# Turning x and B to tokens by VectorE and DRAM instead of TensorE in a hybrid Mamba-2 layer

## The chip, the cores and the metric

The kernel runs on one core of a Trainium2 chip. The metric is the device time of one execution in microseconds. A core has TensorE (PE), VectorE (DVE), ScalarE (ACT), GpSimd (POOL) and SyncE (SP); each works through its own queue of instructions in order. SyncE, ScalarE and GpSimd also issue the DMAs, each from its own queue.

## The reference

One layer of a hybrid decoder on 320 tokens (a new sequence of 256 and 8 continued sequences of 8), in float32. The model width is 2048. A mixer runs two head groups side by side on one input projection, a gated MLP over chunks of 128 tokens and a state-space part (SSD) of 32 heads in four groups; then comes a convolutional feed-forward part of width 5632.

```python
proj = rms_norm(x) @ w_in            # [gate u | gate v | z | x, B, C | dt]
xbc = silu(causal_depthwise_conv(xbc))            # x: 2048 columns, B and C: 4 groups x 128
xdt = x * dt                                      # (tokens, heads, 64)
cb = einsum("bctgn,bcsgn->bctsg", C, B)
y_diag = einsum("bctgr,bcsgrp->bctgrp", cb * decay, xdt)
states = einsum("bcsgn,bcsgr,bcsgrp->bcgrpn", B, decay_states, xdt)
# states of the chunks and the given initial states are chained with their decays
y_off = einsum("bctgn,bcgrpn,bctgr->bctgrp", C, states_in, exp(da_cs))
y = (y_diag + y_off + d_skip * x) * silu(z)       # then a norm over each group
x = x + rms_norm(concat(gate_out, y) @ w_out)
x = x + rms_norm(conv_ffn(rms_norm(x)))
```

The products over tokens (`states`, `y_diag` and the update of each continued sequence's state) need x·dt and B with tokens on the partitions. The projections deliver x, B and C with channels on the partitions.

## The kernel before

**Weights.** Each weight matrix streams in slabs of 512 KB. `slab` loads one (`wraw`, SyncE, L118), ScalarE rounds it to `whi` (L124), VectorE makes the remainder `wlo` (L125). There are three buffers of each. A slab feeds 24 matmuls of `accumulate`: every fp32 product is done as three products of rounded parts (high·high L153, high·low L154, low·high L155; in the projections of v L144). These matmuls, into the PSUM tiles `ps` (projections) and `pd` (products with `w_out`, `w_down`), make up nearly all of TensorE's work.

**Order.** A scheduler orders every engine's queue by priority. The program runs through the projections in sequence; other work is written as generators in a list `bg`, which are advanced a step at a time between slabs. The sequence is: v; B and C with their convolutions (into `bT`, `cT`: channels by tokens); dt and its sums; x of group 0 (`heads_in(0)`, about 200 to 250 us); the gate stage (`gate_up`, `gate_mix`, about 250 to 430 us, with three products by `w_out`); then the pool `sd` is opened for the SSD. Task `ssd(g)` for each of the four groups g runs in `bg` beside `heads_in(g + 1)`, a product by `w_out` and `heads_out` (about 430 to 750 us). The feed-forward part takes the rest.

**Names around the change.**
- `by_token` (L414): a TensorE transpose of 128x128 by the identity into PSUM. For B there are 16 at the start of `sd` (`bt_ps`), for x 16 in each group (`xt_ps`): two chunks of 128 prompt tokens and two halves of the 64 sample tokens, with four blocks of channels each.
- `fourfold` (L418): a ScalarE copy that repeats 32 sample tokens four times along the free axis, so that the transpose has them on all four partition blocks.
- `btok`, `bsp`: B by tokens for the prompt and, split into two rounded parts, for the samples; written from PSUM by ScalarE (and L807 on VectorE for the remainder).
- `times` (L845): VectorE multiplies x by tokens, from PSUM, by dt into `xdt` and `xq`; `decayed` (L851): POOL multiplies by the decay into `xde`; `xsp` (L862, L863): the samples' x·dt in two rounded parts.
- `with_c(i)` (L908): eight matmuls that multiply state i's two tiles (loaded by `load_state`, SyncE, L830, 256 KB each) by C into `yo_ps`; `shrunk` (POOL, L919) then decays the state, `picked` (ScalarE) selects B of the sequence, `grown` multiplies B and `xsp` (TensorE, L925, `up_ps`) and adds the product to the state (VectorE, L927), `store_state` writes it out. States 0 to 3 are visited one after the other, so `with_c` stands in four places of TensorE's order.
- `decays` and `products`: the masks (tiles `cs`, three buffers, L993) and the matmuls of `y_diag` and `y_off` (`y_ps`, L1004); `final`: the prompt's last state (`fin_ps`, L1032).
- `tp` tag "pv": four buffers of 128x320, shared by several steps that evict PSUM.
- the VectorE adds into `acc_mix` (L249) empty the PSUM tiles `pd`, and so free them for TensorE.

Of the kernel before, what the change touches and what calls it, by code (L numbers as in the profile page):

```python
# [9 lines left out]
F32 = mybir.dt.float32  # L10
# [3 lines left out]
ALU = mybir.AluOpType  # L14
# [3 lines left out]
P = 128  # L18
NP = 256
# [15 lines left out]
def hybrid_step(  # L35
# [21 lines left out]
    def misc(name):  # L57
        return ms.tile([P, 512], F32, tag="ms", name=name)
# [114 lines left out]
    def finish(task):  # L173
        while task in bg:
            tick()
# [233 lines left out]

    TOK = ((0, P), (P, P), (NP, NS))  # L410

    def by_token(ps, x, c):

        pe.transpose(ps, x[:, P * c:P * c + P], ident)  # L414

    def fourfold(out, x, i):

        act.copy(out.rearrange("p k (q t) -> p k q t", q=4), x[:, :, NP + 32 * i:NP + 32 * i + 32].unsqueeze(2).to_broadcast([P, 4, 4, 32]))  # L418
        return out

    with ExitStack() as mctx:
        op = mctx.enter_context(tc.tile_pool(name="op", bufs=1))
# [153 lines left out]
        with tc.tile_pool(name="gp", bufs=1) as gp:  # L576
# [193 lines left out]
            conv_proj(B0, 16, lambda j: bT[:, j, :], rooms[0])  # L770
            conv_proj(C0, 20, lambda j: cT[:, j, :], rooms[1])
            bg.append(tasks)
            x0 = heads_in(0, rooms[0])
            finish(normed)
            uf = gate_up(0)
            for g in range(4):
                res = []
                mix = gate_mix(g, uf, res)
                bg.append(mix)
                if g < 3:  # L780
                    uf = gate_up(g + 1)
                    finish(mix)
                    chunk_out(w_out, g, *res, g == 0)
# [4 lines left out]
        with tc.tile_pool(name="sd", bufs=1) as sd:  # L788
# [4 lines left out]
            cb, cms = shared[:, :NT + NS], shared[:, NT + NS:].rearrange("p (b i) -> p b i", b=NB)  # L793
            pool.tensor_copy(cb[:NS, :NS], ident[:NS, :NS])
            pool.tensor_copy(cb[NS:, NT:], ident[NS:, NS:])
            for c in range(4):
# [4 lines left out]
                if c < 2:  # L801
                    act.copy(btok[:, c, :], ps)
                else:
                    b = bsp[:, c - 2]
                    act.copy(b, ps)
                    for rs in (slice(32, 64), slice(96, P)):
                        dve.tensor_tensor(out=b[rs], in0=ps[rs], in1=b[rs].bitcast(F32), op=ALU.subtract)  # L807

            def by_head(ap):
                return ap.rearrange("p (h d) -> p h d", d=64)  # L810
# [9 lines left out]
            def ssd(g):  # L820
# [5 lines left out]
                def load_state(i):  # L826

                    st = [sd.tile([P, 512], F32, tag="st", name="st", bufs=6) for _ in range(2)]
                    for h in range(2):
                        sp.dma_start(st[h], state_ssm[4 * h + i, g])  # L830
                    return st
# [8 lines left out]
                sts = [load_state(i) for i in range(3)]  # L840

                xdt = sd.tile([P, 3, 512], F32, tag="xdt", name="xdt", bufs=1)
                def times(out, ps, c, at=slice(0, P), h=slice(0, 8)):
                    n = h.stop - h.start
                    dve.tensor_tensor(out=by_head(out), in0=by_head(ps),  # L845
                                      in1=dt[at, c, h0 + h.start:h0 + h.stop].unsqueeze(2).to_broadcast([at.stop - at.start, n, 64]), op=ALU.mult)

                xsp = sd.tile([P, 2, 512], F32R, tag="xsp", name="xsp", bufs=1)
                def decayed(i, c):
# [3 lines left out]
                    return xde  # L853

                def x_of_samples(i):
                    ps = misc("xt_ps")
                    x4 = fourfold(sd.tile([P, 4, P], F32, tag="xde", name="x4", bufs=2), xs, i)
                    for j in range(4):
                        by_token(ps[:, P * j:P * j + P], x4[:, j], 0)
                    xq = sd.tile([P, 512], F32, tag="xde", name="xq", bufs=2)  # L860
                    times(xq, ps, 3 + i)
                    act.copy(xsp[:, i], xq)  # L862
                    dve.tensor_tensor(out=xsp[64:, i], in0=xq[64:], in1=xsp[64:, i].bitcast(F32), op=ALU.subtract)  # L863
                    for r in range(2):
                        at = slice(64 - 64 * r + 32 * i, 96 - 64 * r + 32 * i)
                        times(xdt[at, 2, 256 * r:256 * r + 256], ps[at, 256 * r:256 * r + 256], 2, at, slice(4 * r, 4 * r + 4))

                for c in range(2):
                    ps = misc("xt_ps")
                    for j in range(4):  # L870
# [25 lines left out]
                ps = misc("s1_ps")  # L896
                pe.matmul(ps, btok[:, 0, bs], x0d, start=True, stop=True)
                s1 = sd.tile([P, 512], F32, tag="s1", name="s1", bufs=1)
                act.copy(s1, ps)

                ps_yo = misc("yo_ps")

# [39 lines left out]

                def begin(i):
                    with_c(i, sts[i])
                    bms[i] = picked(i)
                    shrunk(i, sts[i])

                def end(i, by=act):
# [1 line left out]
                    store_state(i, sts[i], by)  # L950
                    return made

                for i in range(4):
                    if i < 3:
                        begin(i)
                    else:
# [59 lines left out]
                for j in range(5):  # L1016
                    for i in range(2):
# [30 lines left out]
            def heads_out(g, rate, later):  # L1048

                ssq = hp.tile([P, NT], F32, tag="ssq", name="ssq")  # L1050
                y = x_of.pop(g)
# [384 lines left out]
```

## Time and profile before

| | |
|---|---|
| Median of 3 runs | 1774.73 us (1774.29 to 1776.76) |
| Profiled execution | 1774.69 us, span 1773.0 us |
| TensorE clock granted | 0.999 |
| TensorE busy | 1765.1 us (100%) |
| VectorE busy | 1173.7 us (66%) |
| ScalarE busy | 817.9 us (46%) |
| GpSimd busy | 274.5 us (15%) |
| moved by DMA | 290 MB, 164 GB/s |

All times of a profile are in microseconds from the start of the span, and engines are named PE, DVE, ACT, POOL and SP in it; L414 is line 414 of the kernel before. Matmuls overlap: a row gives the time of one from its start to its end, the chain of waits gives what it adds to the path. In a list of waits the columns are the total, the count and the longest. In a table of stretches each engine has its busy time and its count of instructions, and the last three columns are the granted clock, the share of the DMA engines and GB/s. In a row of DMA issues the columns are the count, the size of one and the median time from issue to landing.

### The profile page before, as it was taken

To read this page: it belongs to the slowest core of one execution; us is meant where nothing else is said; L and a number is where in the kernel's file an instruction comes from. 1 tells how busy PE (TensorE), PEld (TensorE's weight loads), DVE (VectorE), ACT (ScalarE), POOL (GpSimd) and SP (SyncE) were. 2 spreads that over 40 slices of the span, in tenths; PEclk is the share of its full clock that TensorE was granted. 3 is DMA by queue.
4 is the path that set the end of the run, shared out by engine and by line. 5 is a ranking of instruction groups with operands and counts; after the bars stand their busy time and mean duration, and the time that the engine had idled before them with its cause. 6 is when DMAs were issued, how large, how long until landed. Compare 5 with 4: busy or idle time off the path is not lost.

```text
span 1773.0 us, 30633 instructions
## 1 busy us (share of the span) xinstructions
PE 1765.1 (100%) x11897; PEld 1711.9 (97%) x11897; DVE 1173.7 (66%) x2015; ACT 817.9 (46%) x1193; POOL 274.5 (15%) x602
## 2 busy tenths in 40 slices
PE   9999999999999999999999999999999999999998
PEld 7789999999999998999999999999999999999998
DVE  7549764657978778678865465656657575656575
ACT  5434555334564556445645334343434343333445
POOL 1202200000331313103211011010102010101004
PEclk9999999999999999999999999999999999999999
DMA  7556645455666666555554554555455544454542
GB/s 261 161 150 171 189 141 159 153 152 182 223 189 195 186 203 188 147 179 158 171 158 147 154 153 148 155 148 153 150 151 158 144 156 145 156 155 145 155 151 102
DMA packets 217297, 290.01 MB, mean 164 GB/s; under 512 B 19264, under 2 KB 146624, under 8 KB 216960
## 3 DMA queue, kind: packets, MB, share of 16 engines
q1 hardware_dynamic: 205424, 268.84, 50.1%
q10 hardware_dynamic: 10016, 14.16, 2.2%
q0 software_dynamic: 1712, 5.05, 1.0%
q8 instruction: 94, 1.54, 0.4%
q14 instruction: 51, 0.42, 0.1%
HBM read 273.17 MB, written 14.84 MB: 162 GB/s over the span
## 4 chain that ended last, share of the span: by engine, by line
PE 98%; DVE 1%; issue 0%; ACT 0%; ACTq 0%; DVEq 0%
PE ps L153 19%; PE ps L154 19%; PE ps L155 19%; PE pd L153 10%; PE pd L155 10%; PE pd L154 10%; PE ps_v L144 7%; PE y_ps L1004 1%; PE up_ps L925 0%; PE sg L752 0%; PE yo_ps L908 0%; PE xt_ps L414 0%; PE early L70 0%; PE x1p L1299 0%; DVE xsp L863 0%
## 5 line engine op out<-in xcount | busy, mean ns | idle before, releaser
L125 DVE TENSOR_TENSOR wlo<-wraw,whi 128x1024 fp32r<-128x1024 f32 (+1 forms) x476 | 582.3, 1223 | 421.4 <-ACT whi L124 419.6
L124 ACT CAST whi<-wraw 128x1024 fp32r<-128x1024 f32 (+1 forms) x475 | 495.1, 1042 | 714.5 <-PE ps L154 381.5
L153 PE MATMUL ps<-h_hi,whi 128*128 128x320 f32 x2268 | 700.6, 309 | 0.0
L154 PE MATMUL ps<-h_lo,whi 128*128 128x320 f32 x2268 | 699.3, 308 | 0.0
L155 PE MATMUL ps<-h_hi,wlo 128*128 128x320 f32 x2268 | 698.9, 309 | 0.0
L153 PEld LDWEIGHTS ps<-h_hi,whi 128*128 128x128 f32 x2268 | 425.7, 188 | 2.5 <-issue 1.6
L154 PEld LDWEIGHTS ps<-h_lo,whi 128*128 128x128 f32 x2268 | 425.8, 188 | 0.7
L155 PEld LDWEIGHTS ps<-h_hi,wlo 128*128 128x128 f32 x2268 | 425.6, 188 | 0.0
L155 PE MATMUL pd<-fhi,wlo 128*128 128x320 f32 x704 | 217.0, 308 | 0.0
L153 PE MATMUL pd<-fhi,whi 128*128 128x320 f32 x704 | 217.0, 308 | 0.0
L154 PE MATMUL pd<-flo,whi 128*128 128x320 f32 x704 | 217.0, 308 | 0.0
L153 PE MATMUL pd<-ohi,whi 128*128 128x320 f32 x448 | 139.1, 310 | 0.0
L155 PE MATMUL pd<-ohi,wlo 128*128 128x320 f32 x448 | 138.4, 309 | 0.0
L154 PE MATMUL pd<-olo,whi 128*128 128x320 f32 x448 | 138.1, 308 | 0.0
L153 PEld LDWEIGHTS pd<-fhi,whi 128*128 128x128 f32 x704 | 132.2, 188 | 0.0
L154 PEld LDWEIGHTS pd<-flo,whi 128*128 128x128 f32 x704 | 132.2, 188 | 0.0
L155 PEld LDWEIGHTS pd<-fhi,wlo 128*128 128x128 f32 x704 | 132.2, 188 | 0.0
L1201 POOL COPY ptf<-pad 128x2 f32<-128x2 f32 x88 | 21.0, 238 | 602.7 <-DVE pad L1189 601.9
L249 DVE TENSOR_TENSOR acc_ffn<-acc_ffn,pd 128x320 f32<-128x320 f32 (+1 forms) x161 | 77.5, 482 | 37.8 <-PE pd L155 36.3
L153 PEld LDWEIGHTS pd<-ohi,whi 128*128 128x128 f32 x448 | 84.1, 188 | 1.6 <-issue 1.0
L154 PEld LDWEIGHTS pd<-olo,whi 128*128 128x128 f32 x448 | 84.1, 188 | 0.3
L155 PEld LDWEIGHTS pd<-ohi,wlo 128*128 128x128 f32 x448 | 84.1, 188 | 0.2 <-issue 0.2
(335 smaller groups left out, 1866.5 us busy)
## 6 DMA issues: line engine op xcount, KB each, us to landing
wraw<-in_ffn_w_up SPq DMA_DIRECT2D x176, 512.0 KB, 3.6
wraw<-in_w_in SPq DMA_DIRECT2D x140, 512.0 KB, 3.8
wraw<-in_ffn_w_down SPq DMA_DIRECT2D x88, 512.0 KB, 3.3
wraw<-in_w_out SPq DMA_DIRECT2D x64, 512.0 KB, 3.4
st<-in_state_ssm SPq DMA_DIRECT2D x32, 256.0 KB, 4.1
out_ssm_state_sample<-st ACTq DMA_DIRECT2D x30, 256.0 KB, 4.1
cs<-dacs_d SPq DMA_DIRECT2D x16, 320.0 KB, 4.7
xr<-in_xT SPq DMA_DIRECT2D x4, 640.0 KB, 4.0
```

The lines of the kernel that those rows point to most:

```text
L124: rounded[:] = [act.copy(hi, raw).ins]
L125: dve.tensor_tensor(out=lo, in0=raw, in1=hi.bitcast(F32), op=ALU.subtract)
L144: made = pe.matmul(out, xi, w[g][wi], start=first and begins, stop=last and ends)
L153: pe.matmul(ps, whi, xhi, start=first, stop=False)
L154: pe.matmul(ps, whi, xlo, start=False, stop=False)
L155: return pe.matmul(ps, wlo, xhi, start=False, stop=last).ins
L249: added_last[:] = [dve.tensor_tensor(out=acc[:, nb, ts], in0=acc[:, nb, ts], in1=ps[:, ts], op=ALU.add).ins]
L1004: pe.matmul(ps[64 * i:64 * i + 64, cols], w(hl), x(hl, m, cpx), tile_position=(0, 64 * i), **flags)
L1201: pool.tensor_copy(ptf[:, k, :], pad[:, 256:258])
```

## The change

x of each group and B are turned to tokens without TensorE. `to_tokens` takes 64 tokens at a time: one VectorE transpose of 32x32 blocks over 128x256 into a "pv" buffer, then four DMAs from GpSimd's queue that write 64 rows of 512 bytes each to a scratch tensor in DRAM (`b_d`, `x_d[g]`). A tensor takes five such pieces, so 5 transposes and 20 DMAs. `from_dram` reads back 128 tokens by 512 channels through GpSimd's queue, for the samples with a broadcast that repeats 32 tokens four times; a tensor takes four such reads of 256 KB. The rows come back in a permuted order of channels, which `in_order` and the access patterns of `times` undo; `times` becomes two VectorE instructions, which read SBUF. `fourfold` and `by_token` go. B and x of group 0 are written during the gate stage, x of groups 1 to 3 directly behind their convolution in `heads_in_next`; the reads of group g + 1 (three of four) are issued behind the products of group g, into `cs` buffers.

In `ssd` the C products of states 0, 1 and 2 and the first chunk's state product (`state_of_prompt`) stand together in one visit; those of state 3 follow in a second one.

```diff
+    b_d = dr.tile([NT, 512], F32, name="b_d")
+    x_d = [dr.tile([NT, 512], F32, name=f"x_d{i}") for i in range(4)]
...
-    def by_token(ps, x, c):
-        pe.transpose(ps, x[:, P * c:P * c + P], ident)
-    def fourfold(out, x, i):
-        act.copy(out.rearrange("p k (q t) -> p k q t", q=4), x[:, :, NP + 32 * i:NP + 32 * i + 32].unsqueeze(2).to_broadcast([P, 4, 4, 32]))
-        return out
+    def to_tokens(x, rows):
+        for o in range(0, NT, NS):
+            t = tp.tile([P, NT], F32, tag="pv", name="turned", bufs=4)[:, :4 * NS].rearrange("p (r f) -> p r f", r=2)
+            dve.transpose(out=t.rearrange("p r (j f) -> p r j f", j=4), in_=x[:, :, o:o + NS].rearrange("p j (r t) -> p r j t", t=32))
+            for i in range(4):
+                pool.dma_start(rows[o:o + NS, P * i:P * i + P].rearrange("(r t) f -> t r f", t=32), t[32 * i:32 * i + 32])
+            yield
+    def from_dram(out, rows, c):
+        o = P * c if c < 2 else NP + 32 * (c - 2)
+        pool.dma_start(out, rows[o:o + P] if c < 2 else rows[o:o + 32].unsqueeze(0).broadcast_to([4, 32, 512]))
+        return out
...
+            b_turned = to_tokens(bT, b_d)
+            bg.append(b_turned)
             x0 = heads_in(0, rooms[0])
             finish(normed)
+            x0_turned = to_tokens(x0, x_d[0])
+            bg.append(x0_turned)
             uf = gate_up(0)
+            finish(b_turned)
+            for c in range(2):
+                from_dram(b_raw[:, c], b_d, c)
+            finish(x0_turned)
...
+            there = {0: [from_dram(room(), x_d[0], c) for c in range(2)]}
             for c in range(4):
-                ps = misc("bt_ps")
-                b4 = bT if c < 2 else fourfold(sd.tile([P, 4, P], F32, tag="xde", name="b4", bufs=2), bT, c - 2)
-                for g in range(4):
-                    by_token(ps[:, P * g:P * g + P], b4[:, g], c if c < 2 else 0)
...
+                b4 = b_raw[:, c] if c < 2 else from_dram(room(), b_d, c)
+                b = btok[:, c] if c < 2 else bsp[:, c - 2]
+                act.copy(b.rearrange("p (j i f) -> p j i f", j=4, f=32), in_order(b4))
...
+                    for r in range(2):
+                        dve.tensor_tensor(out=to[:, r], in0=of[:, r],
+                                          in1=by[:, r].unsqueeze(2).unsqueeze(3).to_broadcast([n, m, 2, 32]), op=ALU.mult)
...
-                for c in range(2):
-                    ps = misc("xt_ps")
-                    for j in range(4):
-                        by_token(ps[:, P * j:P * j + P], xs[:, j], c)
-                    times(xdt[:, c, :], ps, c)
-                    if c == 0:
-                        x0d = decayed(0, 0)
+                x2, x4 = there[g][:2], there[g][2:]
+                sts = [load_state(i) for i in range(3)]
...
+                times(xdt[:, 0, :], x2[0], 0)
+                x0d = decayed(0, 0)
+                x4 += [from_dram(room(), x_d[g], c) for c in range(2 + len(x4), 4)]
+                yield
+                times(xdt[:, 1, :], x2[1], 1)
                 x_of_samples(0)
                 yield
...
-                for i in range(4):
-                    if i < 3:
-                        begin(i)
-                    else:
+                state_of_prompt(x0d)
+                for i in range(3):
+                    begin(i)
+                yield
+                x_of_samples(1)
+                for i in range(2):
+                    bms[i] = picked(i)
+                yield
+                yield
+                for i in range(3):
+                    end(i)
+                    if i < 2:
+                        bms[i + 2] = picked(i + 2)
+                    if i == 0:
                         sts.append(load_state(3))
-                    if i:
-                        end(i - 1)
                     yield
-                    if i == 0:
-                        x_of_samples(1)
-                    yield
+                yield
                 begin(3)
...
+                if g < 3:
+                    there[g + 1] = [from_dram(room(), x_d[g + 1], c) for c in range(3)]
                 x1d = decayed(1, 1)
...
             def heads_in_next(g):
                 x_of[g] = heads_in(g)
+                for _ in to_tokens(x_of[g], x_d[g]):
+                    pass
                 bg.append(tasks[g])
```

More of the change, by code (lines that the diff above doesn't have):

```diff
@@ L795, in hybrid_step, with room @@
             pool.tensor_copy(cb[NS:, NT:], ident[NS:, NS:])
+            def room():
+                return sd.tile([P, 2, NT], F32, tag="cs", name="xt", bufs=3).rearrange("p i n -> p (i n)")[:, :512]
+            there = {0: [from_dram(room(), x_d[0], c) for c in range(2)]}
             for c in range(4):
-                ps = misc("bt_ps")
-                b4 = bT if c < 2 else fourfold(sd.tile([P, 4, P], F32, tag="xde", name="b4", bufs=2), bT, c - 2)
-                for g in range(4):
-                    by_token(ps[:, P * g:P * g + P], b4[:, g], c if c < 2 else 0)
-                if c < 2:
-                    act.copy(btok[:, c, :], ps)
-                else:
[L804 to L807, printed above, removed]
+                b4 = b_raw[:, c] if c < 2 else from_dram(room(), b_d, c)
+                b = btok[:, c] if c < 2 else bsp[:, c - 2]
+                act.copy(b.rearrange("p (j i f) -> p j i f", j=4, f=32), in_order(b4))
+                for rs in (slice(32, 64), slice(96, P)) if c > 1 else ():
+                    h = b[rs].rearrange("p (j i f) -> p j i f", j=4, f=32)
+                    dve.tensor_tensor(out=h, in0=in_order(b4[rs]), in1=h.bitcast(F32), op=ALU.subtract)
             def by_head(ap):
@@ L838, in load_sums, with times @@
                     return cs
-                sts = [load_state(i) for i in range(3)]
                 xdt = sd.tile([P, 3, 512], F32, tag="xdt", name="xdt", bufs=1)
[L843 to L846, printed above, removed]
+                def times(out, x, c, at=slice(0, P), h=slice(0, 8)):
+                    n, m = at.stop - at.start, (h.stop - h.start) // 2
+                    to = out.rearrange("p (j r i f) -> p r j i f", j=m, r=2, i=2)
+                    of = x.rearrange("p (r i j f) -> p r j i f", r=2, i=2, j=4)[:, :, h.start // 2:h.stop // 2]
+                    by = dt[at, c, h0 + h.start:h0 + h.stop].rearrange("p (j r) -> p r j", r=2)
+                    for r in range(2):
+                        dve.tensor_tensor(out=to[:, r], in0=of[:, r],
+                                          in1=by[:, r].unsqueeze(2).unsqueeze(3).to_broadcast([n, m, 2, 32]), op=ALU.mult)
                 xsp = sd.tile([P, 2, 512], F32R, tag="xsp", name="xsp", bufs=1)
@@ L855, in x_of_samples @@
                 def x_of_samples(i):
-                    ps = misc("xt_ps")
-                    x4 = fourfold(sd.tile([P, 4, P], F32, tag="xde", name="x4", bufs=2), xs, i)
-                    for j in range(4):
-                        by_token(ps[:, P * j:P * j + P], x4[:, j], 0)
                     xq = sd.tile([P, 512], F32, tag="xde", name="xq", bufs=2)
-                    times(xq, ps, 3 + i)
+                    times(xq, x4[i], 3 + i)
                     act.copy(xsp[:, i], xq)
@@ L865, in x_of_samples, with state_of_prompt @@
                         at = slice(64 - 64 * r + 32 * i, 96 - 64 * r + 32 * i)
-                        times(xdt[at, 2, 256 * r:256 * r + 256], ps[at, 256 * r:256 * r + 256], 2, at, slice(4 * r, 4 * r + 4))
-                for c in range(2):
-                    ps = misc("xt_ps")
-                    for j in range(4):
-                        by_token(ps[:, P * j:P * j + P], xs[:, j], c)
-                    times(xdt[:, c, :], ps, c)
-                    if c == 0:
-                        x0d = decayed(0, 0)
+                        times(xdt[at, 2, 256 * r:256 * r + 256], x4[i][at], 2, at, slice(4 * r, 4 * r + 4))
+                s1 = sd.tile([P, 512], F32, tag="s1", name="s1", bufs=1)
+                def state_of_prompt(x0d):
+                    ps = misc("s1_ps")
+                    pe.matmul(ps, btok[:, 0, bs], x0d, start=True, stop=True)
+                    act.copy(s1, ps)
+                x2, x4 = there[g][:2], there[g][2:]
+                sts = [load_state(i) for i in range(3)]
                 ps = misc("cb_ps")
@@ L892, in ssd @@
                                       op=ALU.mult)
+                times(xdt[:, 0, :], x2[0], 0)
[3 more added lines that the diff above has]
+                times(xdt[:, 1, :], x2[1], 1)
                 x_of_samples(0)
                 yield
[L896 to L899, printed above, removed]
                 ps_yo = misc("yo_ps")
@@ L1050, in heads_out @@
                 ssq = hp.tile([P, NT], F32, tag="ssq", name="ssq")
[L1051 removed]
+                y = x_of[g]
                 def z_evac(j, ps):
```

5 lines of the change are left out of this document (3 added, 2 removed).

## Prediction

> **What bounds the kernel now.** I read the page's head, its busy times and its chain first, then the list of TensorE's waits, then the stretches in which the change works.
>
> ```profile
> span 1773.0 us, 30633 instructions
> PE 1765.1 (100%) x11897; PEld 1711.9 (97%) x11897; DVE 1173.7 (66%) x2015; ACT 817.9 (46%) x1193; POOL 274.5 (15%) x602
> PE 98%; DVE 1%; issue 0%; ACT 0%; ACTq 0%; DVEq 0%
> L125 DVE TENSOR_TENSOR wlo<-wraw,whi 128x1024 fp32r<-128x1024 f32 (+1 forms) x476 | 582.3, 1223 | 421.4 <-ACT whi L124 419.6
> L124 ACT CAST whi<-wraw 128x1024 fp32r<-128x1024 f32 (+1 forms) x475 | 495.1, 1042 | 714.5 <-PE ps L154 381.5
> ```
> ```profile
> PE early L70 <- DVE ones L66: 1.1, 1, 1.1
> PE spread L302 <- DVE rs_r L286: 0.7, 2, 0.4
> PE up_ps L925 <- DVE xsp L863: 0.5, 2, 0.2
> PE ps L190 <- ACT h_hi L401: 0.2, 1, 0.2
> ```
> ```profile
> 422.00:504.00 82.00, 81.93 (x610) 76.79 (x609) 67.33 (x112) 51.80 (x102) 23.94 (x33) 1.00 0.68 216
> 504.00:595.00 91.00, 90.74 (x660) 86.02 (x659) 72.29 (x130) 53.52 (x104) 22.51 (x32) 1.00 0.62 190
> ```
> TensorE is busy all the time at a granted clock of 1.00, makes 98% of the chain and waits 2.5 us in all, never for a weight. So a TensorE instruction taken away is time taken away, as long as nothing else then comes late. The stretches (columns: length, PE, PEld, DVE, ACT, POOL) are the state-space stages of groups 0 and 1: VectorE is busy 82% and 79%, close behind. The idle time of the two weight lines says how much lateness is covered: ScalarE's rounding waits mostly for TensorE to free a buffer, so a slab is made as soon as there is room, two slabs ahead. A slab is 24 matmuls at 0.147 us, 3.5 us; two are 7.0, less 1.04 + 1.22 for rounding and remainder: some 4.8 us of cover.
>
> **What is taken from TensorE.** Every L414 matmul goes.
>
> ```profile
> L414 PE MATMUL xt_ps<-ident,xs x32: 271/272/273, 433.6 to 684.9; 128*128 128x128 f32 x32
> L414 PE MATMUL xt_ps<-ident,x x32: 270/272/273, 439.7 to 695.4; 128*128 128x128 f32 x32
> L414 PE MATMUL bt_ps<-ident,bT x8: 271/272/273, 425.5 to 426.7; 128*128 128x128 f32 x8
> L414 PE MATMUL bt_ps<-ident,b x8: 272/273/331, 432.6 to 433.5; 128*128 128x128 f32 x8
> ```
> ```profile
> 504.10 0.87 PE xt_ps L414 x8
> ...
> 509.25 0.15 PE ps L155
> 509.40 0.44 PE xt_ps L414 x4
> 509.84 0.86 PE s_ps L897 x2
> 510.70 0.57 PE yo_ps L908 x8
> 511.27 0.34 PE ps L153
> ```
> The rows of the one line say how many (32 + 32 + 8 + 8 = 80), but their 272 ns overlap; the chain gives what one takes of the path, 0.87 / 8 = 0.109 us. 80 × 0.109 = **8.7 us**. The chain shows a second price: the first weight matmul behind a visit of plain fp32 work takes 0.34 us instead of 0.15, so a visit costs about 0.2 us besides its own matmuls. The matmul orders of the two kernels have 38 such visits in the four groups before and 25 after (the C products of states 0 to 2 and the first-chunk state product now stand in one visit, and visits that held transposes alone are gone): 13 × 0.2 = **2.6 us**. The C products themselves (128) and all other matmuls stay. Together 11.3 us; the visits are few and rounded, so 9.5 to 11.5.
>
> **What is added elsewhere.** VectorE gets 25 transposes of 128x256 and pays the multiplications by dt in two halves, 64 instructions for 32. POOL's queue gets 100 writes of 32 KB and 20 reads of 256 KB. ScalarE loses ten fourfold copies.
>
> ```profile
> L312 DVE STREAM_TRANSPOSE turned<-ssq x4: 505/512/514, 539.1 to 767.8; 128x320 f32<-128x320 f32 x4
> L845 DVE TENSOR_TENSOR xdt<-xt_ps,dt x24: 411/426/692, 438.0 to 701.5; 32x256 f32<-32x256 f32 x16, 128x512 f32<-128x512 f32 x8
> ```
> ```profile
> 83.45 0.54 POOL L711 DMA_DIRECT2D lg<-in_gate_ln_g  x1
> ...
> 85.55 0.56 POOL L738 DMA_DIRECT2D bs<-in_gate_b_s  x1
> ```
> ```profile
> st<-in_state_ssm SPq DMA_DIRECT2D x32, 256.0 KB, 4.1
> wT<-in_gate_wT POOLq DMA_DIRECT2D x4, 256.0 KB, 4.3
> w<-in_gate_w POOLq DMA_DIRECT2D x4, 8.0 KB, 3.4
> bias_bc<-in_ssm_dt_bias POOLq DMA_DIRECT2D x1, 16.0 KB, 5.7
> out_ffn_conv_sample<-stg ACTq DMA_DIRECT2D x22, 32.0 KB, 1.5
> ```
> The nearest transpose, 320 columns, took 0.51 us; 256 of them by columns about 0.43 (estimate). 25 × 0.43 = 10.7 us of VectorE, 2.1 in each tensor. The multiplications: 512 columns 0.69, 256 columns 0.42, so 0.16 fixed and 0.26 for each 256; eight halves at 0.42 and eight at 0.29 against 4 × 0.69 + 4 × 0.42 are +1.3 us a group (nothing to 3, as the operands now come permuted and from SBUF). VectorE's stage of group 1 goes from 72.3 to about 75.7 of 91: still under TensorE, so this costs nothing by its sum.
>
> Five issues on POOL stood 0.53 us apart, so the four writes of one transposed tile take 2.2 us to issue and land after some 3.4, POOL's row for small pieces (1.5 at the least, by ScalarE's row of 32 KB, 5.7 at the most, by POOL's slowest row). B and x of group 0 are written in the gate stage:
>
> ```profile
> 253.71 1.23 DVE L125 TENSOR_TENSOR wlo<-wraw,whi 128x1024 fp32r<-128x1024 f32 x1 [2.30 <-ACT whi L124]
> ...
> 262.07 1.22 DVE L125 TENSOR_TENSOR wlo<-wraw,whi 128x1024 fp32r<-128x1024 f32 x1
> ```
> ```profile
> 262.48 0.58 POOL L736 DMA_DIRECT2D wT<-in_gate_wT  x1 [17.45 <-PE sg L753]
> ```
> POOL stands idle there for 17 us; the 42 issues take 42 × 0.54 = 23 us and end near 268, and the next wT load, issued at 262.5 now, goes behind them, 5 us later; in VectorE's new order its masking stands behind the next projection's evictions, so nobody waits. Six transposes there wait for writes four tiles back, 5.6 us after those start and 2.2 us apart, with a wlo behind some; VectorE idles 2.3 us ahead of a wlo now, and with the slabs' cover I cost this at nothing. If the cover is gone it is the slower rival below.
>
> Where the change adds a wait: the transposes write into the four rooms "pv", so the fifth transpose of a tensor waits until the writes of the first are done, and all of VectorE's queue waits behind it: the adds that free TensorE's accumulators, the products' masks, the next wlo. For group 1, whose fifth transpose comes near 482.6 by VectorE's rows:
>
> ```profile
> 485.40 0.49 DVE L249 TENSOR_TENSOR acc_mix<-acc_mix,pd 128x320 f32<-128x320 f32 x1 [0.55 <-PE pd L155]
> 486.33 0.55 DVE L1014 SCALAR_TENSOR_TENSOR xs<-xs,prm,y_ps 128x320 f32<-128x320 f32 x1 [0.44 <-PE y_ps L1004]
> 489.05 0.49 DVE L249 TENSOR_TENSOR acc_mix<-acc_mix,pd 128x320 f32<-128x320 f32 x1 [0.58 <-PE pd L155]
> 490.81 0.49 DVE L249 TENSOR_TENSOR acc_mix<-acc_mix,pd 128x320 f32<-128x320 f32 x1 [0.47 <-PE pd L155]
> 493.21 1.23 DVE L125 TENSOR_TENSOR wlo<-wraw,whi 128x1024 fp32r<-128x1024 f32 x1 [1.91 <-ACT whi L124]
> ```
> The first tile's writes begin near 480.5, so it waits to 480.5 + 2.2 + 3.4 = 486.1: 3.5 us, plus 2.1 for the transposes. The idle time in these rows gives back 0.55 + 0.44 + 0.58 + 0.47 + 1.91 = 3.95, and the slabs' cover of 4.8 holds the rest; only the accumulators have less. I take 0.4 us for each of groups 1 to 3, **1.2 us** (0 to 2 each).
>
> Group 0's start is the other place. The C products of three states in one visit need all six state loads together.
>
> ```profile
> 438.02 0.37 SPq L118 DMA_DIRECT2D wraw<-in_w_in  x1
> ```
> ```profile
> 441.20 0.64 PE L908 MATMUL yo_ps<-st,cb_cms 128*32 128x256 f32 x8
> ```
> The sixth load stands on SP's queue behind a weight load like this one, which waits for VectorE; issued at 438.4 and landing 4.1 us on, it is there at 442.5. The first state's products start at 441.2; with 0.57 us a state, as in the chain, the visit asks for the third near 442.3 (the transposes taken out ahead of it and the state product put in move that little). I take **0.8 us** (0 to 2). ScalarE there waits for the last of the reads of B, issued when the gate stage's rooms come free near 429.4: four issues and 4.3 us after waiting rooms, near 439.5; with 51.8 of 82 us busy it has to catch up: **0.6 us** (0 to 2). For the later groups the reads are issued a group ahead, into rooms that the products have left; nothing waits for them.
>
> Sum against the profiled execution, 1774.69 us (span 1773.0 and 1.7 around it; the median of three runs is 1774.73): 1774.69 − 8.7 − 2.6 + 1.2 + 0.8 + 0.6 = **1766.0 us**.
>
> A rule that speaks against the change: the Trainium skill, "VectorE: DVE Perf Modes", "Rules for kernel authors", gives a 128×128 transpose to TensorE where PSUM will do as its target, since VectorE turns only 32×32 blocks. By it the kernel before would be the better one; here TensorE is the engine without idle time, and the row of 0.109 us on the path is the measure.
>
> **Rivals.**
> *Nothing waits.* The three waits cost nothing: 1774.69 − 11.3 = 1763.4. For it: TensorE waits only 0.5 us in these stages now. Against: covers of 0.8 us or less at group 0.
>
> *The gain is given back.* VectorE and ScalarE bound the stages: fifth transposes at 2 us each and group 0 at 2 + 2 make 10 instead of 2.6: 1763.4 + 10 = 1773.4. For it: writes that land after 5.7 us, and a VectorE busy to 82%, in bursts. Against: the idle time in the rows of group 1.
>
> *Slower: VectorE held through the "pv" rooms.* If one write takes POOL a whole VectorE instruction (1.22 us, the wlo row) instead of 0.54, four take 4.9, the fifth transpose waits 480.5 + 4.9 + 3.4 = 488.8, which is 6.2 and with the transposes 8.3 us against 3.95 of idle time: 4 us for each of three groups, 13. In the gate stage POOL then needs 40 × 1.22 = 49 instead of 22 us, and the last transposes, with the wlo queued behind them, are late by some 10, less 4.8: 5. 1763.4 + 13 + 5 = 1781. It decides from about 0.9 us an issue. Against it: the wT issue at 262.48 took 0.58 us while a remainder with two SBUF inputs ran beside it. The Trainium skill, "SBUF — State Buffer", "SBUF: two separate sides", has this as a trap: POOL writes its queue's descriptors through a port that certain VectorE instructions hold. By it this rival would be the likely one; that row disagrees.
>
> *The removed work does not shorten the path*: it lay in time in which TensorE would otherwise have waited, 1774. Against: the list of waits.
>
> **How the numbers follow.** Forecast 0.52 (1764.5 to 1769), nothing waits 0.13, given back 0.18, slower 0.13, no effect 0.04. A measurement of this kernel can tell about 0.2%, 3.5 us: faster ends at 1771.2, slower begins at 1778.2. The given-back case spreads from 1769 to 1776, so a third of it is still faster. Faster 0.52 + 0.13 + 0.06 = 0.71; slower 0.13; the same 0.16. The range goes from 1762.5, the upper removal of 11.5 with a little, to 1775.0, over the given-back case; the slower rival is left out.
>
> **What would show it.** Right: no L414; TensorE's busy time down by 11; chain pieces "0.57 yo" no longer alone but joined; waits of TensorE in total under 6 us, at yo_ps near 442 and at the first pd or ps behind each fifth transpose. Wrong: VectorE idle before a transpose for over 6 us, POOL's issues over 0.9 us apart, or TensorE waiting for wlo in the gate stage.

## The result and the profile after

The changed kernel took **1813.97 us** (median of 4, 1812.66 to 1816.59) against 1774.99 us beside it: ratio 1.022 (95% interval 1.0202 to 1.0238). It is 39 us slower where 9 us of gain were forecast.

The head of the page, the busy times and the chain, after:

```profile
span 1812.8 us, 30726 instructions
PE 1770.7 (98%) x11817; PEld 1712.1 (94%) x11817; DVE 1199.2 (66%) x2072; ACT 810.9 (45%) x1183; POOL 341.4 (19%) x722
PE 85%; DVE 6%; DMA 5%; POOL 2%; issue 2%; ACT 1%; SPq 0%; DVEq 0%; POOLq 0%; ACTq 0%
```

The 80 matmuls are gone (11,817 for 11,897), but TensorE has 98% of a longer span, and the chain runs over VectorE and DMAs for 11%. What TensorE waits for most, after (total, count, longest):

```profile
PE up_ps L946 <- DVE xsp L881: 15.0, 4, 6.9
PE yo_ps L929 <- DMA st<-in_state_ssm: 8.2, 7, 2.4
PE up_ps L946 <- DVE st L948: 6.2, 4, 3.1
PE y_ps L1032 <- issue: 1.5, 1, 1.5
PE y_ps L1032 <- POOL cpx L1012: 1.5, 1, 1.5
```

Nearly all of it is work of the state-space groups. The same four stretches of time that hold the four groups before, now after the change, where the groups lie later by what was lost so far (length, PE, PEld, DVE, ACT, POOL, clock, DMA share, GB/s):

```profile
422.00:504.00 82.00, 72.38 (x487) 64.92 (x486) 63.79 (x111) 40.29 (x74) 27.86 (x45) 0.94 0.73 209
504.00:595.00 91.00, 85.92 (x611) 80.64 (x610) 73.24 (x132) 46.32 (x85) 30.63 (x45) 0.98 0.64 198
595.00:683.00 88.00, 79.02 (x527) 73.46 (x526) 62.67 (x110) 38.78 (x74) 31.79 (x39) 0.94 0.64 192
683.00:746.00 63.00, 52.17 (x370) 47.00 (x369) 52.09 (x93) 32.52 (x62) 30.55 (x47) 0.92 0.56 165
```

TensorE is idle for 82 + 91 + 88 + 63 less the four busy times, 34.5 us, where the kernel before has 0.6. And a second cost shows in the clock column, which was 1.00 before: 0.94, 0.98, 0.94 and 0.92. By these shares up to 0.06·82 + 0.02·91 + 0.06·88 + 0.08·63 = 17 us are lost to the clock. Idle time and slow clock, less the 11.3 us that the prediction took from TensorE, come to 40 us, about what was measured.

Two places cost most: the start of group 0 and group 3. Matmul by matmul, the weight products of the kernel after lie 12.5, 20.4, 28.1 and 40.7 us behind those before at the ends of the four stretches.

At the start of group 0 the chain after has this piece (start, length, what):

```profile
435.57 11.92 DMA xt<-b_d
```

The second read of B's samples is issued only at 435.57, since there are three rooms and the first must be emptied by `times`; GpSimd's queue after:

```profile
435.57 0.70 POOL L426 DMA_DIRECT2D xt<-b_d  x1 [3.31 <-DVE xdt L867]
```

The read repeats 32 tokens four times and lands after 11.9 us. ScalarE stands with its copy, and the next rounding of weights with it (ScalarE after, idle time in brackets):

```profile
442.82 0.62 ACT L824 CAST bsp<-xt 128x512 fp32r<-128x512 f32 x1 [7.99 <-DMA xt<-b_d]
447.52 0.62 ACT L824 CAST bsp<-xt 128x512 fp32r<-128x512 f32 x1 [4.08 <-DMA xt<-b_d]
```

The loads of SyncE's own queue are late with it. The DMA issues of 430 to 450 us after, and, last row, of 425 to 450 us before (count, size, time to landing):

```profile
st<-in_state_ssm SPq DMA_DIRECT2D x6, 256.0 KB, 12.0
wraw<-in_w_in SPq DMA_DIRECT2D x2, 512.0 KB, 11.3
xt<-b_d POOLq DMA_DIRECT2D x2, 256.0 KB, 11.6
```
```profile
st<-in_state_ssm SPq DMA_DIRECT2D x6, 256.0 KB, 4.0
```

TensorE waits for the states (after), and its stretches of 4 us there show the clock:

```profile
444.75 0.75 PE L929 MATMUL yo_ps<-st,cb_cms 128*32 128x256 f32 x2 [2.44 <-DMA st<-in_state_ssm]
446.56 2.13 PE L929 MATMUL yo_ps<-st,cb_cms 128*32 128x256 f32 x8 [1.05 <-DMA st<-in_state_ssm]
```

```profile
437.00:441.00 4.00, 4.00 (x28) 3.91 (x27) 2.11 (x3) 0.00 (x0) 1.04 (x2) 1.00 1.01 230
441.00:445.00 4.00, 1.56 (x12) 0.29 (x10) 1.37 (x2) 0.62 (x1) 0.00 (x0) 1.00 1.08 157
445.00:449.00 4.00, 2.64 (x10) 0.37 (x8) 0.81 (x2) 1.48 (x2) 0.68 (x1) 0.51 1.00 192
449.00:453.00 4.00, 2.00 (x10) 1.19 (x11) 3.89 (x9) 2.48 (x6) 0.00 (x0) 0.50 0.69 188
453.00:457.00 4.00, 4.00 (x22) 4.00 (x22) 3.94 (x5) 2.38 (x5) 3.70 (x3) 0.71 0.56 177
```

Behind a stretch in which TensorE works 1.56 of 4 us the granted clock falls to half. The last three rows, 0.51, 0.50 and 0.71, are half rate for 3.9, 4.0 and 2.3 us, some 10.2 us in all, so until near 455.3. TensorE has by then worked without a gap since 452.01, for 3.3 us. The Trainium skill, "TensorE: Matmul & The Clock Gate", "Part 1: The HAM clock gate", states half rate after an idle window of about 3.4 us and full rate after as long a busy one; the trace agrees in size on the way back to full rate, but the rate fell here with no single gap above 2.44 us.

In group 3 the longest of the waits for `xsp` stands, the samples' x·dt; these waits, 15.0 us, are TensorE's largest. VectorE's part of it, the six decays that GpSimd works through meanwhile, and TensorE (after):

```profile
736.88 1.43 DVE L881 TENSOR_TENSOR xsp<-xq,xsp 64x512 fp32r<-64x512 f32 x1
```
```profile
730.26 7.50 POOL L940 TENSOR_TENSOR st<-st,tote 128x512 f32<-128x512 f32 x6
```
```profile
738.37 0.79 PE L946 MATMUL up_ps<-xsp,bm 128*128 128x512 f32 x1 [6.90 <-DVE xsp L881]
```

VectorE's multiplications by dt and this remainder take about two to three times as long beside GpSimd's work as alone; the experiments come back to it.

### The profile page after: what moved, and what is told of

The parts are those of the page before. It is cut to its first block, busy times and chain, and to the rows that moved or that the text cites. A ratio compares the mean times of both kernels' runs of the same rounds, so it can differ in the third digit from the quotient of the medians.

```text
span 1812.8 us, 30726 instructions
## 1 busy us (share of the span) xinstructions
PE 1770.7 (98%) x11817; PEld 1712.1 (94%) x11817; DVE 1199.2 (66%) x2072; ACT 810.9 (45%) x1183; POOL 341.4 (19%) x722
## 4 chain that ended last, share of the span: by engine, by line
PE 85%; DVE 6%; DMA 5%; POOL 2%; issue 2%; ACT 1%; SPq 0%; DVEq 0%; POOLq 0%; ACTq 0%
PE ps L153 16%; PE ps L154 16%; PE ps L155 16%; PE pd L153 9%; PE pd L155 9%; PE pd L154 9%; PE ps_v L144 7%; DVE wlo L125 2%; DMA cs<-dacs_d 1%; POOL x_d L420 1%; DVE cv L460 1%; DMA xt<-b_d 1%; DMA xt<-x_d 1%; DVE xdt L867 1%; DMA st<-in_state_ssm 1%
```

## The experiments

Four kernels of the table (marked *) end, in their profiles, with 6.7 to 7.6 us in which no work is visible: SyncE's last barrier waits there for TensorE's sequencer, 7.5 us at once in the changed kernel without reads (first row; total, count, longest) against 0.9 in the kernel before (second row). No run shows why. It lies behind all of the kernel's work, so beside the medians stands the start of the last addition of a weight product in each profile, as its distance from the kernel before (1756.3). A profile is of one execution, which can lie 3 us from the median.

```profile
SPq L1463 <- PEq L1463: 8.3, 2, 7.5
```
```profile
SPq L1432 <- PEq L1432: 1.1, 2, 0.9
```

| kernel | median us | ratio, 95% interval | last addition |
|---|---|---|---|
| changed kernel | 1813.97 | 1.0202 to 1.0238 | +40.6 |
| merged visits alone | 1789.24 | 1.0065 to 1.0095 | +16.8 |
| merged visits, decays spread | 1789.28 | 1.0062 to 1.0092 | +12.7 |
| tokens by DRAM, four visits | 1812.17 | 1.0195 to 1.0225 | +39.2 |
| the same without reads * | 1799.99 | 1.0126 to 1.0156 | +19.6 |
| ... and without transposes, writes | 1785.14 | 1.0048 to 1.0083 | +10.5 |
| ... and without decays | 1768.52 | 0.9950 to 0.9976 | −4.4 |
| changed kernel without reads * | 1803.41 | 1.0145 to 1.0175 | +20.7 |
| changed kernel without decays | 1799.23 | 1.0121 to 1.0155 | +25.6 |
| prompt alone by DRAM * | 1794.70 | 1.0095 to 1.0125 | +15.6 |
| before with multiplications from SBUF | 1784.16 | 1.0039 to 1.0069 | +9.5 |
| the same without decays | 1776.38 | 0.9996 to 1.0015 | +1.6 |
| before without decays | 1773.57 | 0.9979 to 0.9998 | −0.5 |
| before with transposes and writes * | 1790.61 | 1.0072 to 1.0102 | +8.4 |
| changed kernel, plain reads | 1797.74 | 1.0107 to 1.0141 | +23.0 |
| plain reads, four visits | 1797.49 | 1.0114 to 1.0144 | +22.4 |
| changed kernel, two writes a piece | 1818.22 | 1.0228 to 1.0258 | +47.9 |

**Taking parts out.** First the reads, or the decays, out of the changed kernel.

```diff
-        pool.dma_start(out, rows[o:o + P] if c < 2 else ...)
-        return out
+        return bT.rearrange("p j n -> p (j n)")[:, :512]
```


> The changed kernel without the reads from DRAM: where x and B by tokens are wanted, the tile bT stands instead (so the results are not the layer's); the transposes, the writes and all arithmetic stay. Theory R (the reads through GpSimd's queue land after 7 to 12 us and hold ScalarE and VectorE): the 13 us of group 0 and the late samples of the others go, 1763 to 1772. Theory D (VectorE's multiplications by dt, now from SBUF, stand beside six GpSimd decays in a row and take three times as long): the 11 us each of groups 2 and 3 stay, 1785 to 1795.


```diff
                     with_c(i, sts[i])
-                    shrunk(i, sts[i])
```


> The changed kernel without GpSimd's decays of the given states (32 multiplications of 128x512 left out, the states are not decayed). Theory D: the multiplications by dt go back to about 0.42 us, the waits at up_ps go, and only group 0 with its 13 us and the waits on the writes are left, 1785 to 1793. Theory R: at least 1805.

Neither median lies in a range of its theories; both gave something back, neither all: 20 us of last addition for the reads, 15 for the decays. Matmul by matmul, the four stretches lose 12.5, 7.9, 7.7 and 12.6 us in the changed kernel and 3.5, 4.5, 4.8 and 8.0 without the reads: most of group 0's loss goes, as theory R said, and more than half of the others' stays. So there is more than one cause.

**The two halves of the change.** The merged visits alone on the kernel before, with the later updates of the states that go with them, and the way through DRAM alone.

```diff
-                for i in range(4):
-                    if i < 3:
-                        begin(i)
...
+                for i in range(3):
+                    begin(i)
+                yield
+                x_of_samples(1)
```


> The kernel before with the second part of the change alone: C products of states 0 to 2 in one visit, TensorE's transposes kept. If the visits are worth their switches and cost no wait: 1774.7 less 8 visits of 0.2 us, about 1773. If six decays in a row and state loads that are wanted together are themselves a cause of the loss: 1778 to 1790.

> The changed kernel with the C products in four visits as before, the way through DRAM kept. Theory R: nearly all of the loss is left, 1800 to 1815. Theory D, in which the order of the new visits puts the decays beside the multiplications: groups 2 and 3 lose little, 1780 to 1790.

Visits alone: 14 us slower, with nothing of the way through DRAM in it. TensorE's waits in that kernel:

```profile
PE yo_ps L908 <- DMA st<-in_state_ssm: 4.8, 4, 2.2
PE up_ps L925 <- DVE st L927: 3.2, 6, 1.2
PE y_ps L1010 <- issue: 2.0, 1, 2.0
```

The states' loads are late, and where the updates of three states follow one another, TensorE waits for the additions that free their PSUM tiles (`up_ps`). All its waits come to 14.7 us, where the kernel before has 2.5, and over 624 to 631 us the granted clock was 0.52; together that is about the loss. The way through DRAM alone costs 37 us; on top of it the merged visits add 2, perhaps because what they would wait for is late already. Were the six decays in a row the reason? (The edit is shown against the merged visits alone.)

```diff
-                    shrunk(i, sts[i])
+                    if i in (0, 3):
+                        shrunk(i, sts[i])
...
+                shrunk(1, sts[1])
                 yield
+                shrunk(2, sts[2])
                 yield
```


> The merged visits on the kernel before, but the decays of states 1 and 2 a slab and two slabs later, as the visits were before. If six decays in a row are what makes the merged visits cost: 1774 to 1779. If it is the six state loads that are wanted at once, and the later sample products: 1786 to 1790.

1789.28 us, the same; not the decays in a row. (Its profiled execution was the fastest of its four, that of the merged visits alone the slowest; hence the different last additions.) Whether the loads or the later updates weigh more was not told apart.

**The way through DRAM, peeled.** With four visits, first the reads left out (bT stands for them), then also the transposes and writes, then also the decays.

```diff
-        for o in range(0, NT, NS):
+        for o in ():
```


> Way through DRAM with the C products in four visits, the reads left out (the tile bT stands for x and B by tokens). Theory R (the reads are what is late): about 1766, as the transposes' 8.7 us are gone and nothing else waits. Theory W (the waits for the writes through the four rooms hold VectorE) or theory D (VectorE's multiplications from SBUF): 1785 to 1795.

> As the kernel without reads in four visits, and VectorE's transposes and their writes left out too: what is left of the change is that TensorE transposes nothing and that the multiplications by dt read SBUF, in two halves. Theory W: 1764 to 1768. Theory D (VectorE's multiplications with two SBUF operands are held by GpSimd's decays): still above 1775.

> The kernel without transposes, writes and reads, and also without GpSimd's decays of the states. Theory D: 1762 to 1766, and 5 to 15 us less than with the decays. If the decays don't matter: the same as with them within 2 us.

By the last addition: reads 39.2 − 19.6 = 19.6 us, transposes and writes 19.6 − 10.5 = 9.1, and 10.5 + 4.4 = 14.9 between decays and none. Theories R, W and D were each a part; none of the low times that one theory alone would have given came. With everything out the kernel is faster than before by 0.24 to 0.50%: the transposes were on the path.

**Single costs, added to the kernel before.** The multiplications from SBUF, with and without the decays:

```diff
-                    times(xq, ps, 3 + i)
+                    times(xq, still, 3 + i)      # still: bT, 512 columns; times in two halves
```


> The kernel before, with one thing added: the multiplications by dt read an SBUF tile (bT, so the values are not the layer's) in two halves, as in the changed kernel; TensorE's transposes stay and nobody reads them. Theory D alone is enough: plus 10 to 17 us, 1785 to 1792, without any DMA. If D needs the other parts: within 3 us of 1775.

> The kernel before with the multiplications by dt from SBUF (values not the layer's), and without the decays. If those multiplications cost because GpSimd's decays and VectorE hold one another up: within 2 us of the control without decays. If it is VectorE's longer work as such: 8 us above it, as with the decays.

> Control: the kernel before without GpSimd's decays of the given states (they are left out). As TensorE waits only 2.5 us in all there, 1773 to 1776.

From SBUF they cost 9.5 us (8.3 by the medians), a little less than expected; without the decays 1.6 + 0.5 = 2.1 over the control (2.8), just above the 2 expected. So some 5 to 7 us of it appear only when the decays run too. TensorE's waits for `xsp` fall with the decays; first with them, then without (total, count, longest):

```profile
PE up_ps L930 <- DVE xsp L868: 5.8, 3, 3.8
```
```profile
PE up_ps L930 <- DVE xsp L868: 1.8, 1, 1.8
```

Taking TensorE's transposes away gains nothing as long as this wait stands: the kernel peeled down to these multiplications, without the transposes, is at +10.5, this one, with them, at +9.5. The groups of VectorE from 428 to 770 us (count, busy, mean ns), before and in the control without decays, then with the multiplications from SBUF, then the same without decays (two rows), and in the changed kernel:

```profile
L845 DVE TENSOR_TENSOR xq<-xt_ps,dt 128x512 f32<-128x512 f32 x8 | 5.5, 686 | 1.2 <-PE xt_ps L414 1.2
```
```profile
L845 DVE TENSOR_TENSOR xq<-xt_ps,dt 128x512 f32<-128x512 f32 x8 | 5.5, 686 | 2.6 <-PE xt_ps L414 2.6
```
```profile
L849 DVE TENSOR_TENSOR xq<-bT,dt 128x256 f32<-128x256 f32 x16 | 11.7, 758 | 0.1
```
```profile
L849 DVE TENSOR_TENSOR xq<-bT,dt 128x256 f32<-128x256 f32 x16 | 7.0, 468 | 0.1
L849 DVE TENSOR_TENSOR xdt<-bT,dt 128x256 f32<-128x256 f32 x16 | 11.0, 726 | 0.0
```
```profile
L867 DVE TENSOR_TENSOR xdt<-xt,dt 32x128 f32<-32x128 f32 x32 | 14.7, 488 | 5.6 <-DMA xt<-x_d 5.3
L867 DVE TENSOR_TENSOR xq<-xt,dt 128x256 f32<-128x256 f32 x16 | 10.2, 656 | 4.0 <-DMA xt<-x_d 4.0
L867 DVE TENSOR_TENSOR xdt<-xt,dt 128x256 f32<-128x256 f32 x16 | 9.0, 607 | 5.2 <-DMA xt<-x_d 5.1
```

From PSUM the decays make no difference, 686 ns with and without. From SBUF half the columns of `xq` take longer than all of them took from PSUM, until the decays go. `xdt` stays slow, 726 ns without the decays: GpSimd's other multiplications (`xde`, `cpx`, `s`) run beside it. The trace of the changed kernel tells the two cases apart, instruction by instruction: of the multiplications of 128x256, the 19 with no arithmetic of GpSimd beside them took 0.41 to 0.43 us each, the 13 with some 0.95 us in the mean and up to 1.28. The samples' remainder, which always had two SBUF operands, shows the same in the kernel before and in the control without decays:

```profile
L863 DVE TENSOR_TENSOR xsp<-xq,xsp 64x512 fp32r<-64x512 f32 x8 | 8.4, 1045 | 0.2
```
```profile
L863 DVE TENSOR_TENSOR xsp<-xq,xsp 64x512 fp32r<-64x512 f32 x8 | 5.5, 690 | 0.2
```

In one place of the kernel with the multiplications from SBUF, VectorE and then POOL:

```profile
694.48 2.50 DVE L849 TENSOR_TENSOR xq<-bT,dt 128x256 f32<-128x256 f32 x2
```
```profile
694.44 2.26 POOL L924 TENSOR_TENSOR st<-st,tote 128x512 f32<-128x512 f32 x2 [5.81 <-PE yo_ps L913]
```

Each of two multiplications lasts 1.25 us, about as long as a decay beside it (1.13). The Trainium skill, "SBUF — State Buffer", "Who interferes with whom", says that a VectorE instruction with two SBUF inputs contends with a GpSimd instruction that reads SBUF, and that one with at most one, outside VectorE's two-port modes, does not; the rows above agree with both.

The transposes and the writes added, read by nobody:

```diff
+                for _ in to_tokens(x_of[g], x_d[g]):
+                    pass
```


> The kernel before, with VectorE's 25 transposes and the 100 writes added, which nobody reads. Theory W: plus 8 to 12 us, 1783 to 1787, with VectorE idle before each fifth transpose. If the writes cost only beside the others: within 3 us of 1775.

8.4 us by the last addition (the median, 14.7 us up and above the expected range, holds the longer end too). The place that cost most, in group 1's products (VectorE, POOL, TensorE):

```profile
579.90 1.09 DVE L418 STREAM_TRANSPOSE turned<-xs 128x256 f32<-128x256 f32 x3
...
587.41 0.45 DVE L418 STREAM_TRANSPOSE turned<-xs 128x256 f32<-128x256 f32 x1 [4.74 <-DMA x_d<-turned]
```
```profile
579.16 4.26 POOL L420 DMA_DIRECT2D x_d<-turned  x8 [1.56 <-DVE turned L418]
585.04 1.06 POOL L420 DMA_DIRECT2D x_d<-turned  x2 [1.61 <-DMA x_d<-turned]
```
```profile
588.68 0.85 PE L1021 MATMUL y_ps<-cs,xdt 128*64 128x128 f32 x6 [2.38 <-DVE cs L1010]
590.87 1.47 PE L1021 MATMUL y_ps<-cs,xdt 128*64 128x128 f32 x8 [1.33 <-issue]
```

The fifth transpose stands 4.7 us for a room, the masks of the products (`cs`) behind it, and TensorE 2.38 and then 1.33 us. From 589 to 596 us the granted clock is 0.51, which is another 3.4 us: 7.1 of the 8.4 in this one place. The other two fifth transposes of these stages waited 1.1 us and not at all.

**Repairs.** Plain reads in place of the repeat inside one DMA, then with four visits; two writes a piece; and the prompt alone by DRAM (four pieces, no fifth transpose, samples by TensorE as before, four visits).

```diff
-        pool.dma_start(out, rows[o:o + P] if c < 2 else rows[o:o + 32].unsqueeze(0).broadcast_to([4, 32, 512]))
+        for q in (None,) if c < 2 else range(4):
+            pool.dma_start(out if q is None else out[32 * q:32 * q + 32], rows[o:o + (P if c < 2 else 32)])
```


> The changed kernel with each repeated read of 32 tokens done as four plain reads of 64 KB. Theory: the repeat inside one DMA is what makes these reads land after 7 to 12 us; then they land after 4 to 5, and 10 us or more come back, 1795 to 1804. Rival: it is the queue and what runs beside it; then the four extra issues cost and it is 1812 to 1820.

> The way through DRAM with both mended: C products in four visits, plain reads of 32 tokens. From the kernel without reads in four visits (its last product by a weight 19.6 us later than before) and the reads' remainder: 1793 to 1800. If the mended parts add up to the single costs seen on the kernel before (9 and 8 us, less 9 of transposes): 1783 to 1786.

16 us come back, 17.6 by the last addition. The plain reads of x in this kernel land in 4.0 and 3.5 us, those of B at the crowded start in 6.2 instead of 11.6, and the states' loads beside them in 6.9 instead of 12.0 (DMA issues):

```profile
xt<-x_d POOLq DMA_DIRECT2D x8, 256.0 KB, 4.0
xt<-x_d POOLq DMA_DIRECT2D x32, 64.0 KB, 3.5
xt<-b_d POOLq DMA_DIRECT2D x8, 64.0 KB, 6.2
```

With four visits it is the same time, as expected from the kernel without reads; the single costs do not simply add up.

```diff
-            for i in range(4):
-                pool.dma_start(rows[o:o + NS, P * i:P * i + P].rearrange("(r t) f -> t r f", t=32), t[32 * i:32 * i + 32])
+            for r in range(2):
+                pool.dma_start(rows[o + 32 * r:o + 32 * r + 32].rearrange("t (i f) -> i t f", i=4), t[:, r])
```


> The changed kernel with two writes a piece (32 tokens, all 128 partitions, 64 KB) in place of four: 50 issues instead of 100. If GpSimd's time to issue (0.54 us each) makes the fifth transpose wait: 5 to 10 us come back, 1804 to 1809. If it is the landing: 1812 to 1816.

4 us slower, above both expected times: the number of issues is not what the fifth transpose waits for. These writes, twice as large, landed after 4.4 us in the median instead of 3.3. Nor does issuing take longer than it did: GpSimd's writes in the changed kernel from 428 to 770 us (count, busy, mean ns):

```profile
L420 POOL DMA_DIRECT2D x_d<-turned x60 | 31.9, 539 | 12.5 <-DVE turned L418 7.6 <-DMA x_d<-turned 2.3 <-issue 2.3
```

```diff
-        for o in range(0, NT, NS):
+        for o in range(0, NP, NS):
...
```


> Only the prompt's two chunks of x and B go through DRAM (four pieces a tensor, so that no transpose waits for a room; plain reads); the samples keep TensorE's transposes into PSUM, four visits. 40 transposes of 0.109 us go, 4.4 us. Theory R with the samples' repeated reads as the cause: 1770 to 1772. Theory W with the fifth transpose as the cause: the same. If any use of SBUF operands or of GpSimd's queue costs: 1776 to 1790.

Slower than any of the expected times: 15.6 us later at the last addition, with 40 transposes gone and without repeated reads or a fifth transpose. What is left there are the SBUF multiplications of the prompt and POOL's writes, and TensorE waits most for `xsp` (3.2 us), for nothing visible (2.7), for `cpx` (POOL) and for `fourfold` (ACT, 2.4 each); which of them leads was not told apart. No version that does all of the work beat the kernel before.

## Why the prediction was wrong

- **TensorE bounds the kernel, and what is taken away from it is gained:** right in kind, as long as nothing else is late. In the changed kernel 34.5 us of idle time and up to 17 of slow clock, less the 40.6 lost, leave 11 us, about the 11.3 of the sum. With reads, writes and decays out, the kernel ends 3.9 us before the control without decays, though the SBUF multiplications cost it 2.1: some 6 us for a predicted 8.7 and about 1 of switches. Where the rest is stays open.
- **The multiplications by dt, of which the prediction says "this costs nothing by its sum":** the step that failed most plainly. The sum took VectorE's 5.2 us more over four groups, and compared a stage's total with TensorE's. They took 14.7 + 10.2 + 9.0 = 33.9 us instead of 17.3. The 0.42 us for a half was right for one that runs alone; with both operands in SBUF, beside GpSimd's arithmetic, it was 0.95. Put into the kernel before they cost 9.5 us, because TensorE's products for the samples (`up_ps`) then wait for `xsp`. The samples' remainder with its two SBUF operands, 1045 ns in the mean, was the nearer row than one from PSUM.
- **The fifth transpose, 1.2 us:** the wait was foreseen, its size was not: all transposes and writes cost 8.4 us alone, 7.1 of them at one fifth transpose. The writes were let land 5.6 us after the first issue; there they took 8.2 (579.16 to 587.41). And the sum took VectorE's idle time for slack, in a stage where masks and additions are wanted in order.
- **The visits, some 1.6 of the 2.6 us of gain, and 0.8 for the sixth load:** wrong in sign, 14 us of loss alone, though only 2 on top of the rest. The switches were counted; that three states' loads, products and PSUM tiles are wanted together was priced at one place only.
- **The reads, 0.6 us:** a term of 17.6. The landing of 4.3 us was taken from a plain load. A read that repeats 32 rows landed after 6 to 12 us. And the queue of rooms (three, for four reads of B and x in group 0) was overlooked: the four issues put near 429.4 came from 430.5 to 435.6. That nothing waits for the later groups' reads was wrong as well: group 3's first two were issued at 715.8, and its fourth only at 721.2; in all groups VectorE's multiplications waited 14.4 us for reads (5.3 + 4.0 + 5.1 in the rows above).
- **The price of a wait:** the sum let each microsecond of TensorE's waiting cost one. The granted clock fell to half behind such waits, up to 17 us of the result.
- **The signs of being wrong:** none of the three came. VectorE's longest wait before a transpose was 3.7 us, POOL's issues stayed at 0.54 us, and TensorE waited for no weight in the gate stage. The sign of being right, waits under 6 us in total, failed: the five rows of waits shown above are 32 us alone.
- **The rivals:** "given back" had the kind of loss and a fifth of its size, 10 us of waits against some 50 of idle time and slow clock. The slower rival had the fifth transpose, but not its reason: issues on POOL stayed at 0.539 us in the mean, so VectorE did not hold them up here. What did get held up was VectorE's arithmetic with both operands in SBUF.
- The single costs, 9.5 + 8.4 + 16.8 + 17.6 less 6 to 11 gained, come to 41 to 46, for 40.6 seen. They overlap, and how is open.

## What to carry to other kernels

In a kernel whose bound engine is 100% busy, a change that frees it by 0.5% has to be checked against the order in which the next engine delivers, not against that engine's total. Moving an operand of VectorE from PSUM to SBUF was not free where GpSimd computed from SBUF beside it: look in the profile for the same form with both operands in SBUF, and split its times by what ran beside. And gaps in TensorE's work can cost more than their length: here 34.5 us of idle time came with 17 us of slow clock.

## What the hardware showed that was not expected

- A read of 32 rows with a repeat of four inside one DMA landed after 6 to 12 us, plain reads of 64 KB after 3.5 (x) and 6.2 (B); and loads on another queue landed after 12.0 instead of 4.0 us beside it. The trace has 192 DMA packets of 8 bytes for each of the ten repeated reads, and none in the kernel with plain reads; whether they are what takes the time is not shown.
- The granted clock fell to 0.50 after gaps of 2.44 and 1.05 us with little work between them, not only after one long idle time. Its five stays at half in these stages lasted 10.2, 3.4, 3.4, 6.8 and 10.2 us.
- GpSimd issued eight writes back to back (4.26 us), and then waited 1.61 us for a write to land before the next.
- Four of these programs end with some 7 us in which the last barrier waits for TensorE's sequencer, after all of the work.
